# The masked-decay product of a chunked state-space scan: two heads as two 64-column tiles of TensorE's array, in place of zero-padded 128-column weights

## The chip, the cores and the metric

One core of one Trainium2 chip runs the whole program. The metric is the device time of one execution in microseconds (us); the lower, the better. Engines are named as in the profile: PE is TensorE (PEld its weight loads), DVE is VectorE, ACT is ScalarE, POOL is GpSimd, SP is SyncE, which issues nearly all DMAs.

## The reference, cut to what matters

The reference is one layer of a hybrid backbone: a mixer with two branches (a gated linear recurrence, LRU, and a chunked state-space scan, SSD, both in two directions), merged by gates, then a gated MLP with a 3x3 depthwise convolution. The change lies in the SSD branch, in the part of a chunk's outputs that comes from the chunk's own inputs:

```python
# q = 128 tokens a chunk, 8 chunks, 32 heads of 64 channels in 4 groups
decay_in = jnp.exp(segsum(da))
cb = jnp.einsum('bclgn,bcsgn->bgcls', cc, bc)
y_diag = jnp.einsum('bgcls,bgrcls,bcsgrp->bclgrp', cb, decay_in, xdt)
...
y_off = jnp.einsum('bclgn,bcgrpn,bgrcl->bclgrp', cc, prev, jnp.exp(da_cs))
y = (y_diag + y_off).reshape(bsz, seqlen, nh, hp)
```

## The kernel before, in words

Channels lie on partitions, 128 to a tile, and the 1024 tokens along the columns. The large products (`gdense`, L124) split both operands into two parts of type fp32r and take three matmuls of 128x512 for each 128 rows of the contraction. They make nearly all of the program, in all its stages: the LRU stage, then the SSD stage (about 520 to 1230 us of the profile), the merge, and the MLP.

In the SSD stage 16 tiles j of 128 channels, two heads each, go through two generators that are woven together: `ssd_front(j + 1)` makes the next tile's inputs with L124's products, `ssd_back(j)` does the scan of tile j. A scheduler of the framework turns this into one order for each engine; the program text only sets priorities. `ssd_back` consists of:

- `ssd_decay(j, hf)`: for half hf of the tokens (4 chunks c) and each head h, the masked decay matrix `m[:, h, c, :]`, source token on partitions, target token along the columns, both directions in one.
- `ssd_tokens(j)`: the channels xs are transposed on PE (L907, 8 transposes) into PSUM tiles of 4 chunks, and ACT copies them out to `xt`, the tokens on partitions. `xt` has one buffer for all tiles. From it DVE makes `xw`, weighted for the states, which L931 and L932 multiply with `btok`.
- `ssd_y(j, hf)`: the outputs of one half. L982 multiplies `m` with `xt` into `psy`: for each chunk 128 channels by 128 tokens. L990 multiplies the states `S` with `CT`. DVE adds everything into y.

The weights of a PE product are the 128 channels of `xt`; each head has its own `m`, so the two heads can't be one matmul. Before, `xt` has room for two heads of 128 columns, `[NC, 2, P]`; head 0 fills columns 0 to 63 of its room, head 1 columns 64 to 127 of its own, and POOL fills the rest with zeros once (L707). Each head's product then covers all 128 rows of `psy`, and the second adds to the first:

```python
nc.tensor.matmul(psy[:, c, :], self.xt[:, c0 + c, h, :], m[:, h, c, :],
                 start=(h == 0), stop=(h == 1))
```

All of `m`, `xt`, `S` and `CT` are plain fp32, and a plain fp32 product stands in the trace as two pairs of a weight load and a matmul, a product of fp32r as one. Elsewhere in the program, `ada_row` (L314, before 80 us) multiplies with weights of 2 columns, and `token_rs` (L198) sums with a moving operand of one column.

Of the kernel before, what the change touches and what calls it, by code (L numbers as in the profile page):

```python
# [45 lines left out]
class Builder:  # L46
# [28 lines left out]

# [1 line left out]
    def wload(self, src, n=1024, kn=8):  # L77
# [19 lines left out]
    def drain(self):  # L97
        """ahead of the rest: the products wait for this room"""
        return self.tc.high_priority() if self.DRAIN else nullcontext()

    def queue_weights(self, order, ahead):
        """weights in the order of their products; each is loaded `ahead` products early"""
        self.worder, self.wnext, self.wahead, self.wready = order, 0, ahead, {}
# [24 lines left out]
    def halves(self):  # L128
        """room for a product in two halves, from either kind of PSUM tiles in turn"""
        self.turn = not self.turn  # L130
        if self.turn:
            ps = self.t(self.psD, T, "d")
            return [ps[:, :H], ps[:, H:]]
        return [self.t(self.psS, H, "s") for _ in range(2)]

    @staticmethod
    def weave(main, side, ratio):
        """emit `ratio` steps of side for each step of main"""
        acc = 0.0
        nm = ns = 0  # L140
        for _ in main:
            nm += 1
            acc += ratio
            while acc >= 1.0 and side is not None:
                acc -= 1.0
                if next(side, "end") == "end":
                    side = None
                else:
                    ns += 1
        if side is not None:  # L150
            for _ in side:
                ns += 1
        return nm, ns
# [21 lines left out]
    def rsqrt(self, pool, ps, n, inv, tag):  # L175
        """(ps * inv + EPS) ** -0.5 with one Newton step, for few columns"""
        nc = self.nc
        v = self.t(pool, n, tag + "v")
        a = self.t(pool, n, tag + "a")
        r = self.t(pool, n, tag + "r")  # L180
        nc.vector.tensor_scalar(v, ps, inv, EPS, op0=ALU.mult, op1=ALU.add)
        self.act(a, v, AF.Sqrt)
        nc.vector.reciprocal(r, a)
        self.tt(a, r, r)
        self.tt(a, a, v)
        nc.vector.tensor_scalar(a, a, -0.5, 1.5, op0=ALU.mult, op1=ALU.add)
        self.tt(r, r, a)
        return r

    def token_rs(self, pool, parts, n, inv, tag, ps=None):  # L190
        """parts [128, n tokens]: (inv * sum over partitions and parts + EPS) ** -0.5, the tokens on partitions"""
        nc = self.nc
        nch = n // P
        if ps is None:
            ps = self.t(self.psS, nch, "s")
        for c in range(nch):
            for i, q in enumerate(parts):
                nc.tensor.matmul(ps[:, c : c + 1], q[:, c * P : (c + 1) * P], self.ones[:, 0:1],  # L198
                                 start=(i == 0), stop=(i == len(parts) - 1))
        return self.rsqrt(pool, ps[:, :nch], nch, inv, tag)  # L200

    def spread(self, pool, r, out, tag):
        """out[p, c * 128 + t] = r[t, c] for every p"""
        nc = self.nc
        for c in range(r.shape[1]):
            dg = self.t(pool, P, tag + "dg")
            nc.vector.tensor_scalar(dg, self.ident, r[:, c : c + 1], None, op0=ALU.mult)
            nc.tensor.matmul(out[:, c * P : (c + 1) * P], self.ones, dg, start=True, stop=True)

    def log1p01(self, e, d, s, q):  # L210
        """log1p(e) for e in [0, 1], by atanh's series; d, s, q are room for it"""
        nc = self.nc
# [9 lines left out]

# [1 line left out]
    def dt_chain(self, get, x, L, chunk):  # L224
# [32 lines left out]
    def to_tokens(self, src, nch, dst, halves, scale=1.0):  # L257
        """src [128 (d, hf, h), nch * 128] -> dst [128 token, (hf) nch, 16 pair, 4 (d, h2)]"""
        nc = self.nc
# [8 lines left out]

    # ------------------------------------------------------------------ phases
    def setup(self, cpool):  # L270
# [23 lines left out]
    def lam_chain(self, cpool, pool):  # L294
        """-4 * log_sigmoid(lambda) and 8 * log_sigmoid(lambda)"""
        nc = self.nc
# [13 lines left out]
    def ada_row(self, pool, w, scc):  # L310
        """shift and scale of one tile of channels as rows, for x (row 0) and ctx (row 1)"""
        ps = self.t(self.psS, 256, "s")
# [13 lines left out]
    def ada_direct(self, pool, b, w):  # L326
        """the same, the channels on partitions from the start"""
        for s in range(2):
# [10 lines left out]
    def ada_rest(self, p1):  # L339
        """the other shifts, scales and gates, for x alone"""  # L340
        nc, A = self.nc, self.A
# [14 lines left out]
    def modulate(self, t, src, rs, xh, xl, scale, shift):  # L356
        """(src * rs) * scale + shift, split; t is room"""
        self.stt(t, src, scale, rs, op0=ALU.mult, op1=ALU.mult)
        self.act(xh, t, AF.Identity, bias=shift)
        self.stt(xl, t, shift, xh.bitcast(F32), op0=ALU.add, op1=ALU.subtract)  # L360
# [120 lines left out]
    def first(self, cpool):  # L481
        """context, its SSD states, and the LRU branch"""
        nc, tc, A = self.nc, self.tc, self.A
# [121 lines left out]
    def lru_front(self, j):  # L605
        """context in columns 0:256, latents behind"""
        nc, A, p1, p2 = self.nc, self.A, self.q1, self.q2
# [84 lines left out]
    def ssd(self):  # L692
# [6 lines left out]
        with tc.tile_pool(name="sc1", bufs=1) as q1, tc.tile_pool(name="sg1", bufs=1) as g1, \  # L699
# [4 lines left out]
            etb = self.t(q1, [64, NC], "etb")  # L704
            self.xt = self.t(q1, [NC, 2, P], "xt")
            for h in range(2):
                nc.gpsimd.memset(self.xt[:, :, h, 64 - 64 * h : 128 - 64 * h], 0.0)  # L707
            self.tok = (dtt, cst, wtt, cs_d, etb)
# [49 lines left out]
    def load_R(self, j, hf):  # L758
        """the sums of decays for the channels of each head"""
        self.R = self.t(self.p1, [2, H], "R")  # L760
# [7 lines left out]
    def gates_of(self, j):  # L768
        """the gates made with tile j, and after the last tile"""
        mid = 16 - self.EARLY - self.LATE  # L770
# [124 lines left out]
    def ssd_tokens(self, j):  # L895
# [7 lines left out]
        for hf in range(2):  # L903
            ps = self.t(self.psS, [4, P], "s")
            for c in range(4):
                cc = hf * 4 + c
                nc.tensor.transpose(ps[:, c, :], xs[:, cc * P : (cc + 1) * P], self.ident)  # L907
            for h in range(2):
                q = slice(h * 64, h * 64 + 64)
                self.act(xt[:, hf * 4 : hf * 4 + 4, h, q], ps[:, :, q], AF.Copy)  # L910
            yield
        xw = self.t(p1, [2, NC, P], "xw")
        for d in range(2):
            for h in range(2):
                q = slice(h * 64, h * 64 + 64)
                self.tt(xw[:, d, :, q], xt[:, :, h, q],
                        wtt[:, :, j, 2 * d + h : 2 * d + h + 1].to_broadcast([P, NC, 64]))
            yield
        st.update(S=S, xw=xw)

    def ssd_states(self, j):
        """states entering the chunks: direction 0 by rising chunk, direction 1 by falling chunk"""
        nc = self.nc
# [17 lines left out]
    def ssd_decay(self, j, hf):  # L941
        """m: what the inputs of a chunk add to its outputs, both directions in one"""
        dtt, cst = self.tok[:2]
# [25 lines left out]
    def ssd_y(self, j, hf):  # L969
        """outputs of one half of the tokens, the channels on partitions"""  # L970
        nc, p1, p2 = self.nc, self.p1, self.p2
# [8 lines left out]
        for c in range(4):  # L980
            for h in range(2):
                nc.tensor.matmul(psy[:, c, :], self.xt[:, c0 + c, h, :], m[:, h, c, :], start=(h == 0), stop=(h == 1))  # L982
            if c % 2:
# [36 lines left out]
    def merge(self, pA, pM):  # L1020
        """m[k] = ga * (A @ lru_proj) + gb * (B @ ssd_proj), then @ w_out and the first residual."""
        nc, tc, A = self.nc, self.tc, self.A
# [60 lines left out]
    def sumsq(self, pool, ssq, x, m):  # L1083
        """adds to ssq; the last square stays apart"""
        n = x.shape[-1]
# [11 lines left out]
    def norm(self, parts, n, apply, wait):  # L1097
        """1 / rms of n tokens on all partitions, then apply(k, rs) for each tile of channels"""
        p1, p2 = self.p1, self.p2
# [119 lines left out]
    def tail(self, mh, ml, pA, pM, out):  # L1219
        """w_out, first residual and second norm; the channel sub-layer; final norm"""  # L1220
        nc, tc = self.nc, self.tc
# [63 lines left out]
def host_layout(i):  # L1285
    """Host side: slices, transposes and zero padding only."""
    f = lambda a: np.ascontiguousarray(a)
# [69 lines left out]
```

## Time and profile before

| | |
|---|---|
| median of 3 runs | 2357.77 us (2351.71 to 2358.16) |
| profiled execution, span from the first to the last instruction | 2358.4 us |
| PE busy | 2301.8 us, 98% |
| DVE busy | 1617.5 us, 69% |
| ACT busy | 1067.5 us, 45% |
| POOL busy | 3.4 us |
| queue of nearly all DMAs | 249.90 MB, 32.5% of 16 engines |
| chain that ended last | PE 78%, DVE 11%, DMA 5%, ACT 4% |

The profile is one execution, and gives its span alone; its own time is that span, and what lies around it is not listed. Busy time is the union of an engine's instructions. Matmuls are pipelined: their recorded lengths overlap, and their ends are modelled, so a pace is read from starts. "Idle before" is the time for which the engine stood still ahead of a group, with what ended it.

### The profile page before, as it was taken

The page shows a single profiled execution, that of the slowest core. Times are in us where ns is not written, and L with a number is a line of the kernel's source. Part 1 is how long each engine was busy: PE and PEld are TensorE (multiplying, and loading weights), DVE is VectorE, ACT ScalarE, POOL GpSimd, SP SyncE. Part 2 cuts the span into 40 slices and gives each one's busy share as a digit, 9 for nine tenths or more (in the row PEclk, how much of TensorE's full clock was granted, in tenths as well). Part 3 has the DMA queues.
Part 4 walks back from the last instruction along what each step waited for, and adds up shares of the span by engine and source line. Part 5 has one row for each costly group of instructions (what it writes and reads, how often), then busy time and mean ns, then how long its engine had stood idle before and what let it go on. Part 6 is the DMA issues. An engine that isn't in the chain of part 4 may idle for free.

```text
span 2358.4 us, 29544 instructions
## 1 busy us (share of the span) xinstructions
PE 2301.8 (98%) x11530; PEld 1926.7 (82%) x11530; DVE 1617.5 (69%) x2618; ACT 1067.5 (45%) x1633; POOL 3.4 (0%) x16
## 2 busy tenths in 40 slices
PE   7999999999999999999999999999999999999998
PEld 3778878778888888888888878888888888888888
DVE  4877877889978858668876675557765267436655
ACT  4477667677766546646635232333221122112221
POOL 0000000000000000000000000000000000000000
PEclk8999999999999999999999999999999999999999
DMA  6212222144435333423428675532111111111112
GB/s 249 98 60 81 86 83 70 59 128 148 131 100 160 114 119 110 150 83 133 148 92 272 224 240 186 165 100 72 45 53 42 54 49 44 47 53 54 45 54 72
DMA packets 81455, 251.79 MB, mean 107 GB/s; under 512 B 9730, under 2 KB 15906, under 8 KB 76068
## 3 DMA queue, kind: packets, MB, share of 16 engines
q1 hardware_dynamic: 81312, 249.90, 32.5%
q8 instruction: 91, 1.49, 0.3%
q14 instruction: 48, 0.39, 0.1%
q10 hardware_dynamic: 4, 0.01, 0.0%
HBM read 222.33 MB, written 27.54 MB: 106 GB/s over the span
## 4 chain that ended last, share of the span: by engine, by line
PE 78%; DVE 11%; DMA 5%; ACT 4%; issue 2%; DVEq 0%; SPq 0%; ACTq 0%
PE d L124 37%; PE s L124 28%; PE s L982 2%; PE s L990 2%; DMA adar<-in_ada 2%; ACT L L162 2%; PE s L656 2%; DVE wlo L159 1%; DMA gk<-gd 1%; DVE L L159 1%; PE s L931 1%; PE s L932 1%; PE s L314 1%; DVE L L156 1%; DMA raw<-in_w 1%
## 5 line engine op out<-in xcount | busy, mean ns | idle before, releaser
L124 PE MATMUL d<-H,whi 128*128 128x512 f32 x2464 | 690.4, 398 | 1.2 <-ACT whi L162 1.0
L124 PEld LDWEIGHTS d<-H,whi 128*128 128x128 f32 x2464 | 450.6, 188 | 88.7 <-ACT whi L162 1.9
L162 ACT ACTIVATE whi<-raw 128x1024 fp32r<-128x1024 f32 (+1 forms) x194 | 203.2, 1049 | 581.5 <-PE s L124 347.5
L124 PE MATMUL d<-H,wlo 128*128 128x512 f32 x1232 | 385.9, 392 | 0.4 <-DVE wlo L159 0.3
L159 DVE TENSOR_TENSOR wlo<-raw,whi 128x1024 fp32r<-128x1024 f32 (+1 forms) x194 | 234.2, 1209 | 204.3 <-ACT whi L162 201.4
L124 PEld LDWEIGHTS d<-H,wlo 128*128 128x128 f32 x1232 | 230.2, 188 | 49.2 <-DVE wlo L159 1.7
L124 PE MATMUL s<-A,whi 128*128 128x512 f32 x960 | 258.4, 389 | 0.0
L124 PE MATMUL d<-A,whi 128*128 128x512 f32 x960 | 258.3, 389 | 0.0
L124 PE MATMUL s<-H,whi 128*128 128x512 f32 x832 | 251.3, 390 | 0.2 <-ACT whi L162 0.2
L156 DVE SCALAR_TENSOR_TENSOR facc<-d,vec,facc 128x945 f32<-128x945 f32 (+5 forms) x184 | 216.7, 1178 | 11.2 <-ACT facc L162 5.9
L124 PEld LDWEIGHTS d<-A,whi 128*128 128x128 f32 x960 | 180.1, 188 | 37.6
L124 PEld LDWEIGHTS s<-A,whi 128*128 128x128 f32 x960 | 180.2, 188 | 37.3
L124 PEld LDWEIGHTS s<-H,whi 128*128 128x128 f32 x832 | 155.9, 188 | 33.2 <-ACT whi L162 0.7
L162 ACT ACT_TABLE_LOAD x107 | 137.3, 1283 | 76.3 <-DVE cacc L156 28.7
L124 PE MATMUL s<-H,wlo 128*128 128x512 f32 x416 | 157.1, 390 | 2.8 <-DVE wlo L159 2.8
L156 DVE SCALAR_TENSOR_TENSOR M<-s,mods,M 128x512 f32<-128x512 f32 (+1 forms) x72 | 49.6, 690 | 160.7 <-PE s L124 160.5
L124 PE MATMUL d<-A,wlo 128*128 128x512 f32 x480 | 149.2, 389 | 0.2 <-DVE wlo L159 0.2
L124 PE MATMUL s<-A,wlo 128*128 128x512 f32 x480 | 149.1, 389 | 0.0
L124 PEld LDWEIGHTS d<-A,wlo 128*128 128x128 f32 x480 | 90.0, 188 | 19.2 <-DVE wlo L159 0.6
L124 PEld LDWEIGHTS s<-A,wlo 128*128 128x128 f32 x480 | 90.1, 188 | 18.7
L162 ACT ACTIVATE m<-GU,dtt 128x128 f32<-128x128 f32 x256 | 78.9, 389 | 48.5 <-PE s L982 43.5
L156 DVE SCALAR_TENSOR_TENSOR m<-GL,dtt,m 128x128 f32<-128x128 f32 x256 | 77.0, 345 | 29.5 <-ACT m L162 29.0
(274 smaller groups left out, 3191.4 us busy)
## 6 DMA issues: line engine op xcount, KB each, us to landing
raw<-in_w SPq DMA_DIRECT2D x92, 512.0 KB, 3.6
E<-csd SPq DMA_DIRECT2D x32, 1024.0 KB, 4.9
raw<-in_wup SPq DMA_DIRECT2D x44, 512.0 KB, 3.4
R<-csd SPq DMA_DIRECT2D x64, 256.0 KB, 3.9
adar<-in_ada SPq DMA_DIRECT2D x32, 512.0 KB, 4.3
gated<-sg SPq DMA_DIRECT2D x32, 256.0 KB, 2.5
gd<-y SPq DMA_DIRECT2D x32, 256.0 KB, 4.4
gk<-gd SPq DMA_DIRECT2D x32, 256.0 KB, 3.7
```

The lines of the kernel that those rows point to most:

```text
L124: nc.tensor.matmul(o, a[:, k, :], b[k][:, xo + s : xo + e], start=(k == 0 and i == 0), stop=(k == kn - 1 and i == 2))
L156: self.nc.vector.scalar_tensor_tensor(out, in0, s, in1, op0=op0, op1=op1)
L159: self.nc.vector.tensor_tensor(out, a, b, op=op)
L162: self.nc.scalar.activation(out, in_, f, **kw)
L314: self.nc.tensor.matmul(ps[:2, :], scc[:, k, :], w[:, k, :], start=(k == 0), stop=(k == 7))
L656: nc.tensor.matmul(pg, a[:, q, :], b[:, s:e], start=(i == 0), stop=(i == 2))
L931: nc.tensor.matmul(ps[:, s - s2, 0, :], btok[:, s, :], xw[:, 0, s, :], start=True, stop=True)
L932: nc.tensor.matmul(ps[:, s - s2, 1, :], btok[:, 7 - s, :], xw[:, 1, 7 - s, :], start=True, stop=True)
L982: nc.tensor.matmul(psy[:, c, :], self.xt[:, c0 + c, h, :], m[:, h, c, :], start=(h == 0), stop=(h == 1))
L990: nc.tensor.matmul(pso[:, c, :], S[:, cc if d == 0 else 7 - cc, d, :], CT[:, cc * P : (cc + 1) * P], start=True, stop=True)
```

## The change

It puts each head's product on its own half of the array's columns. `xt` shrinks to `[NC, P]`, the two heads side by side, without zeros. Head 0's product has the 64 columns 0 to 63 as weights and writes partitions 0 to 63 of `psy`, head 1's has columns 64 to 127 and writes partitions 64 to 127; neither adds to the other (both start and stop). The framework derives the tile of the array from the operands: 128 rows by 64 columns, at column 0 and at column 64. The copies of `xt` out of PSUM and the products for `xw` no longer go head by head. The changed file also has no comments and docstrings, and from `ssd_y` on its line numbers are 5 lower (L982 becomes L977, L990 becomes L985).

```diff
@@ def ssd
-            self.xt = self.t(q1, [NC, 2, P], "xt")
-            for h in range(2):
-                nc.gpsimd.memset(self.xt[:, :, h, 64 - 64 * h : 128 - 64 * h], 0.0)
+            self.xt = self.t(q1, [NC, P], "xt")
@@ def ssd_tokens
-            for h in range(2):
-                q = slice(h * 64, h * 64 + 64)
-                self.act(xt[:, hf * 4 : hf * 4 + 4, h, q], ps[:, :, q], AF.Copy)
+            self.act(xt[:, hf * 4 : hf * 4 + 4, :], ps, AF.Copy)
             yield
         xw = self.t(p1, [2, NC, P], "xw")
         for d in range(2):
-            for h in range(2):
-                q = slice(h * 64, h * 64 + 64)
-                self.tt(xw[:, d, :, q], xt[:, :, h, q],
-                        wtt[:, :, j, 2 * d + h : 2 * d + h + 1].to_broadcast([P, NC, 64]))
+            self.tt(xw[:, d].rearrange("p c (h q) -> p c h q", h=2), xt.rearrange("p c (h q) -> p c h q", h=2),
+                    wtt[:, :, j, 2 * d : 2 * d + 2].unsqueeze(3).to_broadcast([P, NC, 2, 64]))
             yield
@@ def ssd_y
         for c in range(4):
             for h in range(2):
-                nc.tensor.matmul(psy[:, c, :], self.xt[:, c0 + c, h, :], m[:, h, c, :], start=(h == 0), stop=(h == 1))
+                q = slice(h * 64, h * 64 + 64)
+                nc.tensor.matmul(psy[q, c, :], self.xt[:, c0 + c, q], m[:, h, c, :], start=True, stop=True)
             if c % 2:
                 yield
```

The scheduler makes a new order from this. The number of PE instructions stays the same, 10,568 in the program; ACT has 37 fewer (32 copies, 5 table loads), DVE 32 fewer, POOL 2 fewer, and SP the same 604 DMAs. On PE, the 256 products stand in 36 uninterrupted groups before and after: 28 groups of 8 products, and 4 pairs of groups of 4.

PE, a group of 8 in the middle of the SSD stage (`d` is the PSUM tile of a large product, `s` one of a small product, the shape is that of the output). Before:

```order
2481 L932 MATMUL s_7392<-xw_7274,btok_7091 128x128
2482 L124 MATMUL d_7457<-H_128_481,whi_1037_7296 128x512
2483 L982 MATMUL s_7399<-m_1016_7127,xt_3595 128x128 x8
2484 L124 MATMUL d_7457<-H_129_482,whi_1037_7296 128x512
2485 L990 MATMUL s_7415<-bc_987_6893,S_7258 128x128 x4
```

The same group after the change:

```order
2476 L926 MATMUL s_7354<-xw_7238,btok_7057 128x128
2477 L124 MATMUL d_7419<-H_122_441,whi_1037_7258 128x512 x2
2478 L124 MATMUL d_7419<-H_123_442,whi_1037_7258 128x512
2479 L977 MATMUL s_7361<-m_1016_7093,xt_3595 64x128 x8
2480 L124 MATMUL d_7419<-H_123_442,whi_1037_7258 128x512
2481 L124 MATMUL d_7419<-H_122_441,wlo_1038_7259 128x512 x2
2482 L124 MATMUL d_7419<-H_128_481,whi_1037_7258 128x512
```

The group still stands between two matmuls of L124, that is between products on the whole array; the states' product behind it (L990, now L985) comes three matmuls later.

PE, one of the four places where the group is in two parts. Before:

```order
2408 L124 MATMUL d_7084<-H_122_441,wlo_1000_7020 128x512 x2
2409 L982 MATMUL s_7177<-m_970_6716,xt_3595 128x128 x4
2410 L124 MATMUL d_7084<-H_128_481,whi_999_7019 128x512 x2
2411 L124 MATMUL d_7084<-H_129_482,whi_999_7019 128x512 x2
2412 L124 MATMUL d_7084<-H_128_481,wlo_1000_7020 128x512 x2
2413 L982 MATMUL s_7177<-m_970_6716,xt_3595 128x128 x4
2414 L990 MATMUL s_7193<-bc_809_5256,S_6683 128x128 x4
```

After:

```order
2406 L124 MATMUL d_7050<-H_122_441,wlo_1000_6986 128x512 x2
2407 L977 MATMUL s_7143<-m_970_6682,xt_3595 64x128 x4
2408 L124 MATMUL d_7050<-H_128_481,whi_999_6985 128x512 x2
2409 L124 MATMUL d_7050<-H_129_482,whi_999_6985 128x512 x2
2410 L124 MATMUL d_7050<-H_128_481,wlo_1000_6986 128x512 x2
2411 L977 MATMUL s_7143<-m_970_6682,xt_3595 64x128 x4
2412 L985 MATMUL s_7159<-bc_809_5238,S_6653 128x128 x4
```

Here nothing moved: the two parts stay apart, with the same six matmuls of L124 between them.

## Rows read from the trace of the kernel before

**Rows 1.** The page: span, busy time by engine, PE and its clock by slices.
```profile
span 2358.4 us, 29544 instructions
...
PE 2301.8 (98%) x11530; PEld 1926.7 (82%) x11530; DVE 1617.5 (69%) x2618; ACT 1067.5 (45%) x1633; POOL 3.4 (0%) x16
...
PEclk8999999999999999999999999999999999999999
```
**Rows 2.** Busy time by stretch: PE, PEld, DVE, ACT, POOL, then granted clock, DMA, GB/s.
```profile
520.00:1230.00 710.00, 707.14 (x3952) 609.06 (x3951) 559.22 (x1250) 434.49 (x819) 0.00 (x0) 1.00 0.39 125
...
43.50:58.50 15.00, 15.00 (x74) 7.87 (x73) 10.61 (x18) 5.36 (x9) 0.00 (x0) 1.00 0.72 255
```
**Rows 3.** Waits of PE and PEld, 520 to 1230 us: total us, times, longest.
```profile
PE s L931 <- DVE xw L159: 2.8, 2, 2.2
...
PEld s L931 <- PE d L124: 3.0, 10, 0.9
PEld s L931 <- issue: 2.6, 1, 2.6
```
**Rows 4.** Groups, 520 to 1230 us: count, busy us, mean ns, idle before and releaser.
```profile
L982 PE MATMUL s<-m,xt 128*128 128x128 f32 x512 | 63.0, 275 | 0.0
...
L159 DVE TENSOR_TENSOR xw<-xt,wtt 128x512 f32<-128x512 f32 x60 | 39.0, 681 | 0.0
...
L159 DVE TENSOR_TENSOR m<-m,E 128x1024 f32<-128x1024 f32 x31 | 37.7, 1217 | 0.2
...
L162 ACT ACTIVATE xt<-s 128x256 f32<-128x256 f32 x60 | 19.6, 375 | 23.9 <-PE s L907 23.9
...
L162 ACT ACTIVATE btok<-s 128x512 f32<-128x512 f32 x6 | 3.3, 595 | 1.7 <-PE s L845 1.7
```
**Rows 5.** Timeline of weight loads around one group: start us, length us, engine, line.
```profile
898.52 1.86 PEld L982 LDWEIGHTS s<-m,xt 128*128 128x128 f32 x16
900.30 0.19 PEld L124 LDWEIGHTS d<-H,whi 128*128 128x128 f32 x1
```
**Rows 6.** Timeline around L198: loads, then one of the matmuls.
```profile
884.21 0.41 PEld L124 LDWEIGHTS d<-H,wlo 128*128 128x128 f32 x2
884.75 1.00 PEld L198 LDWEIGHTS s<-ones,ssq 128*128 128x128 f32 x8
885.67 0.77 PEld L124 LDWEIGHTS d<-H,whi 128*128 128x128 f32 x4
...
884.43 0.62 PE L124 MATMUL d<-H,wlo 128*128 128x512 f32 x2
```
**Rows 7.** Timeline of PE where L314 and L124 alternate.
```profile
44.47 3.62 PE L314 MATMUL s<-adaw,scc 128*2 128x256 f32 x16
48.02 0.60 PE L323 MATMUL s<-ident,row 2*128 2x2 f32 x4
...
50.40 0.73 PE L124 MATMUL d<-H,whi 128*128 128x512 f32 x2
51.06 0.59 PE L314 MATMUL s<-adaw,scc 128*2 128x256 f32 x2
51.59 0.73 PE L124 MATMUL d<-H,whi 128*128 128x512 f32 x2
52.25 1.02 PE L314 MATMUL s<-adaw,scc 128*2 128x256 f32 x4
53.21 0.73 PE L124 MATMUL d<-H,whi 128*128 128x512 f32 x2
```
**Rows 8.** L864 and L982, each line's loads: length ns min/median/max, first and last start.
```profile
L864 PEld LDWEIGHTS s<-ident,grsr x4: 84/84/84, 686.1 to 1242.6; 128*8 128x8 f32 x4
...
L982 PEld LDWEIGHTS s<-m,xt x512: 186/192/192, 522.1 to 1226.3; 128*128 128x128 f32 x171
```
**Rows 9.** The chain in order of time: start, us, line and count.
```profile
1441.14 10.88 PE d L124 x48
```
**Rows 10.** Timeline of weight loads at one switch, idle time before in brackets.
```profile
51.06 0.09 PEld L314 LDWEIGHTS s<-adaw,scc 128*2 128x2 f32 x2 [0.37 <-issue]
```

## The prediction

> **What bounds the kernel now.** I read the page first: TensorE (PE) is busy for 2301.8 of 2358.4 us, and its clock digits stand at 9 nearly throughout [rows 1]. A busy PE is not proof that PE is the bound, so the next view is the stretch in which the changed lines run. All of L982, L907's copies and the xw products lie between 520 and 1230 us. There PE is busy for 707.14 of 710 us at a granted clock of 1.00, which is the 2.4 GHz level, VectorE (DVE) for 559 and ScalarE (ACT) for 434 [rows 2]. The third view is the waits of PE in that stretch: the reader is to see that the matmuls waited twice on DVE's xw, 2.8 us in all, and the loads of L931 for 5.6 us more, in pieces [rows 3]. So in this stage a microsecond of PE work taken away or added is a microsecond of the end, until DVE (79% busy) becomes the bound. Behind the stage lie about 1130 us of other products, which the change does not touch.
>
> **What one group costs before.** The groups of instructions give L982 512 matmuls of 128x128 [rows 4], and its line 512 weight loads [rows 8]. The program has 256 such products (16 tiles, 2 halves, 4 chunks, 2 heads), so each fp32 product is recorded as two pairs of a load and a matmul. The recorded lengths (275 and 192 ns) overlap, so I take the pace from starts: 16 loads from 898.52 to 900.30 us, 0.111 us per pair [rows 5]. The whole product costs 512 x 0.111 = 56.8 us of PE.
>
> What sets 0.111? Two things at once. L198 has the same 128-column load and a matmul of a single column, and still goes 8 pairs from 884.75 to 885.67, 0.115 each [rows 6]: the load alone sets the pace. L314 is the reverse, 2 columns of weights and 256 columns streamed: groups of 2, 4 and 16 take 0.53 (51.06 to 51.59), 0.96 (52.25 to 53.21) and 3.55 us (44.47 to 48.02) [rows 7]; the slope, (3.55 - 0.53) / 14, is 0.216 us for 256 columns, so 0.108 for 128. Load and stream both take what is seen, and halving the load alone gains next to nothing. The clock was 1.00 there too [rows 2].
>
> **The change, part by part.**
> (a) The product. After the change each load has 64 columns. Of the load I take half of 0.111, 0.056 us; the lengths of an 8-column and a 128-column load, 84 and 192 ns [rows 8], are 0.9 ns a column apart, which says 0.053. The stream still has 128 columns, 0.108 us. So everything hangs on whether the two heads, now on two halves of the columns, stream side by side. The trace has no two matmuls on different column tiles; the bounds are full overlap and none. In the order of the program each chunk is head 0 twice, then head 1 twice. If a matmul waits only for its own half, the second of head 0 runs beside the first of head 1, and the second of head 1 beside the first of the next chunk: two streams' time a chunk, 0.216 us, against four loads, 0.224. Paced by the loads, 512 x 0.056 = 28.7 us, and at the end of each of 36 groups the last stream sticks out by 0.05, 1.9 us: 30.6, a gain of 26.2. Without overlap it is 512 x 0.108 = 55.3, a gain of 1.5. I take full overlap, because nothing in the rows makes the second half wait and the loads ran under the streams in L314's small tile, 16 in the 3.55 us that the streams alone explain [rows 7].
>
> The Trainium skill has a measurement for this in TensorE: Matmul & The Clock Gate, Part 3, "Measured speedup vs the span model": three column tiles at 2.38 times the pace of one. No run here shows it; for two tiles it would give nearly the sum above.
>
> (b) The switches. L982's groups now use half the array's columns at a time, the products around them all of it. The trace has such switches where L314 (2 columns of weights) alternates with L124. From the first L124 matmul at 50.40 to the first at 51.59 us are 1.19 us [rows 7]; a 512-column matmul takes 10.88 / 48 = 0.227 us [rows 9], so two of these and two of L314 are 0.886, and 0.304 is left. The next round, 51.59 to 53.21 with four of L314, leaves 1.62 - 0.454 - 0.864 = 0.302. The row of loads shows why: L314's load begins at 51.06 together with its matmul, and the loader sat idle before it [rows 10]; between products of one kind the load is ahead, L124's at 884.21 for a matmul at 884.43 [rows 6]. L864 looks like a counter-example (8 columns, no gap), but it is a transpose and its compiled load still names the whole array, so it prices nothing. To 0.304 I add the 64-column load that is now exposed on entering, 0.056: 0.36 us for in and out. The order lists 36 groups, before and after, each with full-array products on both sides: 36 x 0.36 = 13.0 us lost. The bounds are nothing (a switch that falls where the loader waits anyway) and these 13.0.
>
> (c) xt is copied out of PSUM by one ACT instruction of 512 columns for each half, not two of 256. Before, 4 x 0.375 us for each tile; a 512-column copy takes 0.595 (btok) [rows 4], so 1.50 becomes 1.19, 5.0 us of ACT over 16 tiles. The order has 5 table loads fewer as well. xw is two DVE instructions of 1024 instead of four of 512: 4 x 0.681 = 2.72 becomes 2 x 1.217 = 2.43 [rows 4], 4.6 us. PE hides both: ACT and DVE are at 61% and 79% of the stage [rows 2], and the one wait of PE that this can shorten is the 2.8 us on xw [rows 3]. I count nothing. If the cover goes (PE gains 26 us) DVE's share is still 555 of 684 us, 81%. POOL's two fills of xt lie before the stage and nobody waits for them. The DMAs are the same 604; on SP the scheduler moves R and E loads by a few places, and E's lateness costs ACT time that PE does not see.
>
> **Sum.** -26.2 + 13.0 = -13.2 us against the profiled execution's span of 2358.4, so 2345. The median of the runs, 2357.77, stands 0.03% under that span; I make no correction.
>
> **The rivals.**
> *No overlap.* The heads stream one after the other: -1.5 + 13.0 = +11.5 us, 2370. This is slower, by one mechanism, the switches around 36 groups; it decides as soon as the overlap saves under 13.0 us, 0.36 us for each of the 36 groups. It is also the case in which the change doesn't do what it says. For it: no row shows two tiles at once. Against it: nothing in the rows ties the halves together.
> *Half overlap.* If a load only begins when the matmul before it has started (in [rows 5] loads and matmuls keep one pace), head 1's first matmul starts 0.056 after head 0's second, and its own second a stream later: 2 x (0.108 + 0.056) = 0.328 a chunk, 42.0 us for 128 chunks, a gain of 14.8 and a net -1.8: 2357, no change. For it: loads and matmuls pair off one to one in the rows. Against it: a half that is free could be loaded earlier.
> *Free switches.* Full overlap, and the gap hidden by waits that the loader has anyway: -26, 2332. Against it: both rounds of [rows 7] give the gap, 0.304 and 0.302.
> *Exposed loads.* In the tile mode the load no longer runs under the stream: 512 x (0.108 + 0.056) = 84.0, +27.2, and with the switches +40, 2398. Against it: L314's 16 in 3.55 us. The Trainium skill, in the same page's Part 3, "The mechanism", says loads overlap running matmuls only where the row groups differ; both heads use all rows, so by that rule this rival would come true. L314's row group is also all rows and its loads are hidden, so the trace disagrees, though its loads are of 2 columns.
>
> **How the numbers follow.** Full overlap 0.42, half overlap 0.24, no overlap 0.20, free switches 0.09, exposed loads 0.05. The likeliest gives 2345; its own range, with switches between a third and all of their price and the loads at 0.053 to 0.06, is 2335 to 2348. For 8 in 10 the range runs from 2333 (nearly free switches) to 2372 (no overlap, with 2 us for the moved order). A measurement of this kernel can tell about 0.3%, 7 us, from no change. Faster by more: most of full overlap and free switches, 0.46. Within: half overlap mostly, with edges of its neighbours, 0.28. Slower: no overlap and exposed loads, 0.26.
>
> **What would show each step.** In the changed profile L982's line has become L977, with 512 matmuls of 64 columns of weights. The starts of a group of 16 decide: 0.9 us and what the switch adds for full overlap, 1.3 for half, 1.73 for none, 2.6 for exposed loads. A load after a group (L124's) that begins some 0.2 us after the last L977 matmul started, not with it, shows the switch; the pair costs 0.36 us if I am right. PE must still be busy throughout 520 to 1230, and the stage shorter by 13 us; a new wait of PE on xw, S or m there, or a stage that ends earlier with the end unmoved, would make the forecast wrong in another way.

## The result and the profile after

The changed kernel takes 2339.78 us in the median of 4 runs (2339.40 to 2342.84), the kernel before 2357.40 in 4 runs beside them: a ratio of 0.9936 (95% interval 0.9922 to 0.9950), 17.6 us in the medians. Two later sets of runs gave 2340.69 (0.9926, 0.9915 to 0.9938) and 2339.57 (0.9929, 0.9913 to 0.9945). The forecast was 2345, its range 2333 to 2372. The profiled execution has a span of 2341.1 us against 2358.4, 17.3 us less.

The page of the changed kernel: span, busy time by engine, the granted clock in 40 slices, and the engines' shares of the chain that ended last.

```profile
span 2341.1 us, 29454 instructions
...
PE 2285.2 (98%) x11530; PEld 1896.3 (81%) x11530; DVE 1613.5 (69%) x2586; ACT 1061.3 (45%) x1596; POOL 2.4 (0%) x14
...
PEclk8999999999999999999999999999999999999999
...
PE 84%; DVE 10%; DMA 3%; ACT 2%; issue 1%; DVEq 0%; ACTq 0%
```

PE has 16.6 us less to do (2301.8 in [rows 1]) and the span is shorter by about as much. So the time was taken from PE's work, and PE still leads the chain (84% of it).

Busy time in the SSD stage, the columns as in [rows 2], and what PE and its loads still waited for there.

```profile
520.00:1230.00 710.00, 707.99 (x4039) 592.68 (x4038) 561.38 (x1231) 434.81 (x794) 0.00 (x0) 1.00 0.41 129
```
```profile
PE s L198 <- DVE ssq L159: 1.0, 1, 1.0
PE s L925 <- DVE xw L159: 0.6, 1, 0.6
...
PEld s L977 <- issue: 11.2, 32, 0.4
PEld d L124 <- issue: 5.3, 31, 0.2
```

PE is as full as before, at a clock of 1.00. No wait of PE on another engine is over 1.0 us. New are the last two rows: the loader stands idle ahead of nearly every group of L977 (11.2 us, 32 times) and ahead of the product behind it (5.3 us, 31 times). These are the switches.

The loads of L977 (length in ns: least, median, most; then first and last start), and the groups of the stage.

```profile
L977 PEld LDWEIGHTS s<-m,xt x512: 132/137/137, 520.2 to 1206.3; 128*64 128x64 f32 x171
```
```profile
L977 PE MATMUL s<-m,xt 128*64 128x128 f32 x512 | 35.9, 280 | 0.0
...
L159 DVE TENSOR_TENSOR xw<-xt,wtt 128x1024 f32<-128x1024 f32 x30 | 36.4, 1222 | 0.6 <-ACT xt L162 0.6
...
L162 ACT ACTIVATE xt<-s 128x512 f32<-128x512 f32 x30 | 17.5, 593 | 29.8 <-PE s L905 29.8
```

From the first load of the product to the last are now 686.1 us, against 704.2 (522.1 to 1226.3) in [rows 8]: 18.1 us, all of the gain, lie in the stage. L977's 512 matmuls cover 35.9 us, L982's covered 63.0 [rows 4]. The copies and xw came out as costed: 593 ns a copy where 595 was taken, 1222 ns an xw product where 1217 was.

What one group costs can be read where it stands in the same company in both kernels, between two and four matmuls of L124. PE's timeline (start us, length us, engine, line, count), before:

```profile
910.94 0.62 PE L124 MATMUL d<-H,wlo 128*128 128x512 f32 x2
911.40 1.95 PE L982 MATMUL s<-m,xt 128*128 128x128 f32 x16
913.10 1.17 PE L124 MATMUL d<-H,whi 128*128 128x512 f32 x4
914.10 0.62 PE L124 MATMUL d<-H,wlo 128*128 128x512 f32 x2
```

After, matmuls and then loads (in brackets the loader's idle time before):

```profile
896.80 0.61 PE L124 MATMUL d<-H,wlo 128*128 128x512 f32 x2
897.34 1.09 PE L977 MATMUL s<-m,xt 128*64 128x128 f32 x16
898.37 1.20 PE L124 MATMUL d<-H,whi 128*128 128x512 f32 x4
899.40 0.62 PE L124 MATMUL d<-H,wlo 128*128 128x512 f32 x2
...
897.34 0.85 PEld L977 LDWEIGHTS s<-m,xt 128*64 128x64 f32 x16 [0.35 <-issue]
898.37 0.76 PEld L124 LDWEIGHTS d<-H,whi 128*128 128x128 f32 x4 [0.17 <-issue]
```

From the first start to the last are 3.16 us before (910.94 to 914.10) and 2.60 after (896.80 to 899.40). Six matmuls of L124, 6 x 0.227 [rows 9], are 1.36 of both, so the group costs 1.80 before and 1.24 after: 0.56 us saved. Within the group the recorded starts after the change come in pairs, 7 ns between the two of a pair; from the first pair to the second are 0.16 us, from there on 0.109 to 0.110 from pair to pair. At 0.110 the 8 pairs are 0.88 us. What is left, 0.36 by these rounded starts and 0.355 as the median over the groups of 16 that have four matmuls of L124 behind them, is the switch: 0.09 us more than usual between L124's last start and L977's first, 0.05 in the longer first step inside the group, and some 0.2 on the way out, where the load of L124 only begins with its own matmul (898.37 both). The experiments below were planned with 0.345.

Over the stage: 28 groups of 16 at a median of 0.564 us make 15.8, 8 groups of 8 at 0.091 make 0.7. That is 16.5 of the 17.3 us.

### The profile page after: what moved, and what is told of

It is laid out like the page before. It is cut to its first block, busy times and chain, and to the rows that moved or that the text cites. A ratio compares the mean times of both kernels' runs of the same rounds, so it can differ in the third digit from the quotient of the medians.

```text
span 2341.1 us, 29454 instructions
## 1 busy us (share of the span) xinstructions
PE 2285.2 (98%) x11530; PEld 1896.3 (81%) x11530; DVE 1613.5 (69%) x2586; ACT 1061.3 (45%) x1596; POOL 2.4 (0%) x14
## 4 chain that ended last, share of the span: by engine, by line
PE 84%; DVE 10%; DMA 3%; ACT 2%; issue 1%; DVEq 0%; ACTq 0%
PE d L124 42%; PE s L124 30%; PE s L985 2%; PE s L656 2%; PE s L977 1%; DVE wlo L159 1%; DVE L L159 1%; PE s L926 1%; DMA adar<-in_ada 1%; PE s L925 1%; ACT L L162 1%; PE s L314 1%; DVE L L681 1%; DMA raw<-in_w 1%; PE s L598 1%
## 5 line engine op out<-in xcount | busy, mean ns | idle before, releaser
L124 PE MATMUL d<-H,whi 128*128 128x512 f32 x2464 | 690.4, 398 | 0.4 <-ACT whi L162 0.2
L124 PEld LDWEIGHTS d<-H,whi 128*128 128x128 f32 x2464 | 451.0, 189 | 93.5 <-issue 6.0
L124 PE MATMUL d<-H,wlo 128*128 128x512 f32 x1232 | 386.5, 393 | 2.0 <-DVE wlo L159 2.0
L124 PEld LDWEIGHTS d<-H,wlo 128*128 128x128 f32 x1232 | 229.9, 188 | 51.5 <-DVE wlo L159 3.7
L124 PE MATMUL s<-A,whi 128*128 128x512 f32 x960 | 258.4, 389 | 0.0
L124 PE MATMUL d<-A,whi 128*128 128x512 f32 x960 | 258.3, 389 | 0.0
L124 PE MATMUL s<-H,whi 128*128 128x512 f32 x832 | 252.5, 391 | 2.7 <-ACT whi L162 2.7
L156 DVE SCALAR_TENSOR_TENSOR facc<-d,vec,facc 128x945 f32<-128x945 f32 (+5 forms) x184 | 216.8, 1178 | 11.2 <-ACT facc L162 5.9
L124 PEld LDWEIGHTS d<-A,whi 128*128 128x128 f32 x960 | 180.2, 188 | 37.6
L124 PEld LDWEIGHTS s<-A,whi 128*128 128x128 f32 x960 | 180.2, 188 | 37.3
L124 PEld LDWEIGHTS s<-H,whi 128*128 128x128 f32 x832 | 156.6, 189 | 36.0 <-ACT whi L162 3.1
L124 PE MATMUL s<-H,wlo 128*128 128x512 f32 x416 | 157.4, 391 | 1.4 <-DVE wlo L159 1.3
L124 PE MATMUL s<-A,wlo 128*128 128x512 f32 x480 | 149.2, 389 | 0.5 <-DVE wlo L159 0.5
L124 PE MATMUL d<-A,wlo 128*128 128x512 f32 x480 | 149.1, 389 | 0.0
L124 PEld LDWEIGHTS s<-A,wlo 128*128 128x128 f32 x480 | 90.0, 188 | 19.5 <-DVE wlo L159 1.0
L124 PEld LDWEIGHTS d<-A,wlo 128*128 128x128 f32 x480 | 90.1, 188 | 18.7
L156 DVE SCALAR_TENSOR_TENSOR E<-E,cst 128x128 f32<-128x128 f32 x256 | 82.3, 349 | 19.5 <-ACT E L162 19.5
```

What stands on the lines that cost most here:

```text
L124: nc.tensor.matmul(o, a[:, k, :], b[k][:, xo + s : xo + e], start=(k == 0 and i == 0), stop=(k == kn - 1 and i == 2))
L156: self.nc.vector.scalar_tensor_tensor(out, in0, s, in1, op0=op0, op1=op1)
```

## The experiments

The theory: the two tiles' streams run side by side (8 stream times for a group of 16 matmuls), each of the 36 groups pays one switch of some 0.35 us, and nothing else counts. Its rivals give the gain to the shorter chains on ACT and DVE, let the two fp32 passes of one product overlap instead of the two heads, or hold that the switches cost nothing. The first four kernels that follow shared one chip and 29 runs of the kernel before (median 2356.41).

### e1: the product alone

The kernel before, with its padded xt, its copies and its xw, and only the product on the tiles:

```diff
-                nc.tensor.matmul(psy[:, c, :], self.xt[:, c0 + c, h, :], m[:, h, c, :], start=(h == 0), stop=(h == 1))
+                q = slice(h * 64, h * 64 + 64)
+                nc.tensor.matmul(psy[q, c, :], self.xt[:, c0 + c, h, q], m[:, h, c, :], start=True, stop=True)
```

> The kernel before with the product alone changed: xt keeps its zero-padded room, its copies and xw go head by head, and only the two matmuls of a chunk take 64 columns each and write 64 partitions. Theory (the two heads' streams run side by side, each group of 16 matmuls in about 0.88 us, less about 0.35 us of switch for each of 36 groups): all of the gain is here, 2340 us give or take 3. Rival (the gain is in the copies, in xw or in the scheduler's new order): 2352 to 2358, as before.

Measured: 2338.05 us (2336.19 to 2344.46), ratio 0.9926 (0.9912 to 0.9939). The groups of this kernel's stage:

```profile
L159 DVE TENSOR_TENSOR xw<-xt,wtt 128x512 f32<-128x512 f32 x60 | 39.3, 684 | 0.0
...
L983 PE MATMUL s<-m,xt 128*64 128x128 f32 x496 | 34.8, 280 | 0.0
L983 PEld LDWEIGHTS s<-m,xt 128*64 128x64 f32 x496 | 26.4, 136 | 12.0 <-issue 10.7 <-ACT m L162 1.1
```

The xw products are the old ones of 512 columns, the matmuls the new ones, and the loader has the same idle time ahead of them. The whole gain is there without the shorter chains on ACT and DVE.

### e2: the copies and xw alone

The changed kernel with the product on the whole array:

```diff
-                nc.tensor.matmul(psy[q, c, :], self.xt[:, c0 + c, q], m[:, h, c, :], start=True, stop=True)
+                nc.tensor.matmul(psy[:, c, :], self.xt[:, c0 + c, :], m[:, h, c, :], start=True, stop=True)
```

> The changed kernel with the product back on the whole array: each head multiplies with all 128 columns of xt, and head 1 overwrites head 0 (so head 0's decay is left out of the result); the compact xt, its single copies and the two xw instructions stay. Theory: no gain without the tiles, 2357 give or take 3, matmuls 0.112 us apart, a load beginning with the last matmul of a group. Rival (copies, xw or order carry the gain): 2340.

Measured: 2354.55 us (2350.37 to 2358.59), ratio 0.9988 (0.9979 to 0.9996), 1.9 us less in the medians. PE's timeline at a group:

```profile
904.08 1.95 PE L976 MATMUL s<-m,xt 128*128 128x128 f32 x16
905.78 1.17 PE L124 MATMUL d<-H,whi 128*128 128x512 f32 x4
```

From 904.08 to 905.78 are 1.70 us, as before the change (911.40 to 913.10). On whole-array products the shorter chains are worth at most a few us: the waits of PE on xw, 2.8 us in [rows 3], were gone in this kernel's stage. But e1 had no such wait either, with the old chains, so the part does not add to the product's.

### e3: all of head 0, then all of head 1

The changed kernel with its two loops exchanged:

```diff
-        for c in range(4):
-            for h in range(2):
-                q = slice(h * 64, h * 64 + 64)
+        for h in range(2):
+            q = slice(h * 64, h * 64 + 64)
+            for c in range(4):
                 nc.tensor.matmul(psy[q, c, :], self.xt[:, c0 + c, q], m[:, h, c, :], start=True, stop=True)
-            if c % 2:
-                yield
+            yield
```

> The changed kernel with the loops of the product exchanged: first head 0 for four chunks, then head 1 for four, the same 64-column tiles and the same number of groups and switches. Theory (overlap needs a matmul of the other tile near in the order): the 16 matmuls go one after the other at 0.109, 1.7 us a group, 2340 + 32 x 0.8 = 2366, slower than before. Rival (two recorded matmuls of one product, not two tiles, run side by side, or the engine fetches the other head's matmuls out of order): 2340, the pairs unchanged.

Measured: 2357.00 us (2353.46 to 2360.95), ratio 1.000 (0.9989 to 1.001): between the two expectations. PE's timeline:

```profile
889.70 1.58 PE L977 MATMUL s<-m,xt 128*64 128x128 f32 x16
891.21 0.50 PE L124 MATMUL d<-H,whi 128*128 128x512 f32 x1
```

From 889.70 to 891.21 are 1.51 us; after the change it was 1.03 (897.34 to 898.37). The order within the group alone takes back the gain: 0.48 us for a group of 16. The starts within this group, in ns from one to the next, are

```
160 109 109 110 5 104 56 53 57 52 57 109 109 109 109
```

Matmuls of one head follow one another a full stream apart (109), so the rival that the two passes of one product overlap is out: the overlap is between the tiles. Eight groups of this kernel hold one head alone; there the starts are 109 or 110 apart throughout, behind a first step of 160, and nothing overlaps: 8 matmuls take the 1.09 us in which the changed kernel has 16.

```profile
655.44 1.09 PE L977 MATMUL s<-m,xt 128*64 128x128 f32 x8
```

But my theory in its strict form is out as well. In the order of the program head 1's first matmul is the ninth; had every matmul waited for the one ahead of it to start, the group's last would start 1.64 us after its first (15 x 0.109), and it starts after 1.31. With eight 109-ns streams on each tile, a body this short needs head 1 to begin beside head 0's fifth, ahead of three that still wait. That is read from the times, since the records do not name the tile. In the middle both run (starts 52 to 57 ns apart), then head 0 runs out, and head 1 finishes alone. So the other half of the rival, that the other head's matmuls are started out of order, holds in part.

### e4: more switches

The states' matmul of one direction is put behind each chunk's two products, so the groups on the tiles become 80 short ones instead of 36, with the same matmuls. Against the changed kernel:

```diff
+        pso = self.t(self.psS, [4, P], "s")
         for c in range(4):
             for h in range(2):
...
+            cc = c0 + c
+            nc.tensor.matmul(pso[:, c, :], S[:, cc, 0, :], CT[:, cc * P : (cc + 1) * P], start=True, stop=True)
```

> The changed kernel with the first states' product of each half (L985, direction 0) put between the chunks of the masked product: in 16 of the 32 halves the order now has four tile groups with a whole-array product between them, 80 groups instead of 36, and no other work. Theory (a switch in and out costs about 0.345 us whatever stands around it): 44 x 0.345 = 15 us more, and 1 to 2 us for streams that lose their partner at a group's end, 2340 + 16 = 2356. Rival (the gaps of rows 7 belong to the early stage, a switch is nearly free here): 2340 to 2343.

Measured: 2355.10 us (2352.03 to 2356.86), ratio 0.9991 (0.9983 to 1.000). PE's timeline (L978 is the product on the tiles, L980 the states' product):

```profile
901.65 0.44 PE L978 MATMUL s<-m,xt 128*64 128x128 f32 x4
902.01 0.49 PE L980 MATMUL s<-bc,S 128*128 128x128 f32 x2
902.43 0.44 PE L978 MATMUL s<-m,xt 128*64 128x128 f32 x4
902.80 0.49 PE L980 MATMUL s<-bc,S 128*128 128x128 f32 x2
903.22 0.44 PE L978 MATMUL s<-m,xt 128*64 128x128 f32 x4
```

A round takes 0.785 us (901.65 to 903.22 is two). Two pairs on the tiles are 0.22, two matmuls of L980 another 0.22, so 0.345 us is the switch in and out. By the times, the kernel is 15.3 us above the changed kernel's 2339.78; over 44 added groups that is 0.35 us each. The two ran on different chips; by the two ratios (0.0055 of 2356.4) it is 0.29, and against e1 on the same chip (2338.05) 0.39. The rival of free switches would have left the time where it was. With 80 groups nearly all of the gain is gone.

### e6 and e7: both halves of a tile in one group

If each switch costs 0.35 us, fewer and longer groups should gain. e6 puts the products of both halves of the tokens together, behind the next tile's first decay, so that 36 groups become 17. m gets a third buffer for that, and y takes psy in before the second direction's states, to save room in PSUM. The diff against the changed kernel, in ssd_back and ssd_y, cut to its core:

```diff
-    BUFS = {"L": 10, "adaw": 3, "raw": 2, "cacc": 4, "csg": 2, "row": 3, "xdg": 4}
+    BUFS = {"L": 10, "adaw": 3, "raw": 2, "cacc": 4, "csg": 2, "row": 3, "xdg": 4, "m0": 3}
...
+            yield from self.ssd_y(j - 1, 0)
             yield from self.ssd_y(j - 1, 1)
...
-        yield from self.ssd_y(j, 0)
...
+        if hf == 0:
+            st["psy"] = {}
+            for g in (0, 1):
+                st["psy"][g] = self.t(self.psS, [4, P], "s")
...
+            self.tt(y, t[:, 1] if d else psy.rearrange("p c q -> p (c q)"), y if d else t[:, 0], op=ALU.add)
```

> The changed kernel with the outputs of both halves of a tile made together, after the next tile's first decay matrix (a third buffer for m; the masked product of 8 chunks stands in one piece; y takes the product's part before the second states' product): 17 groups in the order where there were 36, the same work. Theory (each group pays about 0.345 us for its switches): 19 x 0.345 = 6.6 us less, 2333. Rival (what a group pays is given back elsewhere, or the moved outputs make PE wait): 2339 to 2345.

Measured: 2341.53 us (2338.64 to 2343.61), ratio 0.9929 (0.9917 to 0.9941), against 2340.69 for the changed kernel on the same chip: no gain, a miss. The waits in its stage, the timeline of ACT and PE at one of them, and the busy times and clock there (columns as in [rows 2]):

```profile
PE d L124 <- ACT zs L162: 6.4, 3, 2.7
...
PEld s L981 <- issue: 5.0, 14, 0.4
...
ACT xs L162 <- DVE y L156: 17.9, 8, 4.7
```
```profile
869.21 1.21 ACT L162 ACTIVATE xs<-d,vec 128x1024 f32<-128x1024 f32 x1 [3.58 <-DVE y L156]
...
871.72 1.02 ACT L162 ACTIVATE zs<-d 128x1024 f32<-128x1024 f32 x1
...
872.80 1.24 PE L124 MATMUL d<-H,whi 128*128 128x512 f32 x4 [2.73 <-ACT zs L162]
...
874.70 1.91 PE L124 MATMUL d<-H,whi 128*128 128x512 f32 x4
876.40 1.01 PE L124 MATMUL d<-H,wlo 128*128 128x512 f32 x2
```
```profile
873.00:877.00 4.00, 4.00 (x12) 3.15 (x12) 3.06 (x4) 3.95 (x5) 0.00 (x0) 0.60 0.16 18
```

The switches went as meant: the loader's idle time ahead of the product fell from 11.2 to 5.0 us. But three times PE now waits for ACT, which has to empty a large product's PSUM tile into zs, 6.4 us in all. ACT comes late because ahead of zs, in its own order, it stands idle until DVE has made y (3.58 us here, 17.9 in the stage where the changed kernel has 1.0). That y reads the tile of xs made before, and ACT is about to write the next xs: the later outputs hold xs longer. After the longest of PE's waits the granted clock stands at 0.60 in the mean of the next 4 us: the four matmuls from 874.70 take until 876.40, 0.425 each instead of 0.227. What the fewer switches should have saved, 6.6 us, is about what these waits and the slow matmuls behind one of them took.

e7 has e6's move, with the product on the whole array as in e2, so that there are no switches to save; against e6:

```diff
-                        q = slice(h * 64, h * 64 + 64)
-                        nc.tensor.matmul(st["psy"][g][q, c, :], self.xt[:, g * 4 + c, q], st["m"][g][:, h, c, :],
+                        nc.tensor.matmul(st["psy"][g][:, c, :], self.xt[:, g * 4 + c, :], st["m"][g][:, h, c, :],
                                          start=True, stop=True)
```

> The same move of the outputs with the product on the whole array, as in the run that kept the copies only (head 0's decay is left out of the result). Theory: without tiles there is no switch to save, so the move alone gives nothing, 2353 to 2357. Rival (the move itself helps or hurts): 2347 or less, or 2362 or more.

Measured: 2370.17 us (2366.22 to 2378.27), ratio 1.0053 (1.0039 to 1.0067). Busy times in its stage, and its waits:

```profile
520.00:1230.00 710.00, 699.27 (x3837) 602.55 (x3836) 543.56 (x1183) 409.74 (x763) 0.00 (x0) 0.99 0.38 121
```
```profile
PE d L124 <- ACT zs L162: 6.7, 3, 2.2
PE s L906 <- ACT xt L162: 2.7, 3, 2.2
```

PE stands still for 10.7 of the 710 us, 2.9 before the change [rows 2]; the profile is of the slowest of the six runs (2378.27 us). The theory that the move alone gives nothing failed, and the rival that it hurts holds: 12 us in the medians. The price is not one constant, though: with these 12 us and 6.6 saved e6 would stand 5.8 us above the changed kernel, and it stands 0.8 above. So e6's miss is accounted for by the waits in its own trace; e7 shows that the move can hurt, and neither confirms nor refutes the price of a switch.

### e8: heads in turn, two chunks at a time

e3 suggests that the other tile's matmul must stand near in the order. Here, in the changed kernel, two chunks of head 0 are followed by two of head 1:

```diff
-        for c in range(4):
+        for b in range(0, 4, 2):
             for h in range(2):
                 q = slice(h * 64, h * 64 + 64)
-                nc.tensor.matmul(psy[q, c, :], self.xt[:, c0 + c, q], m[:, h, c, :], start=True, stop=True)
-            if c % 2:
-                yield
+                for c in range(b, b + 2):
+                    nc.tensor.matmul(psy[q, c, :], self.xt[:, c0 + c, q], m[:, h, c, :], start=True, stop=True)
+            yield
```

> The changed kernel with two chunks of head 0, then two of head 1, in turn, so that four recorded matmuls of one tile stand ahead of four of the other. Theory (from the run with four chunks a head, where head 1's first matmul started beside head 0's fifth of eight, past three that still waited): three can be passed, so the tiles still run side by side throughout, 2340 give or take 2. Rival (a matmul of the other tile passes no more than one that waits, and the half overlap of that run has another cause): half of the loss of that run or more, 2348 to 2357.

Measured: 2342.81 us (2340.64 to 2343.83), ratio 0.9933 (0.9920 to 0.9946), on the chip where the changed kernel took 2340.69. PE's timeline:

```profile
896.12 1.15 PE L978 MATMUL s<-m,xt 128*64 128x128 f32 x16
897.20 1.20 PE L124 MATMUL d<-H,whi 128*128 128x512 f32 x4
```

That is 0.8 us above the theory's range and well below the rival's 2348. The group takes 1.08 us to the next start instead of 1.03. Four matmuls of one head in a row, where e3 had eight, are bridged almost wholly. As in e3, waiting matmuls of head 0 are passed by those of head 1.

### e9: both halves together, but not where PSUM ran out

e6's waits fell near 670, 870 and 1070 us, at the tile that begins a new group of heads. e9 leaves tiles 3, 7 and 11 as in the changed kernel: 20 groups. The diff against e6, cut to its core:

```diff
+            if jj:
+                yield from self.ssd_y(j - 1, 0)
...
+        if jj == 3 and j < XS_TILES - 1:
+            yield from self.ssd_y(j, 0)
...
+        apart = j % 4 == 3 and j < XS_TILES - 1
+        if hf == 0 or apart:
+            st["psy"] = {}
+            for g in (hf,) if apart else (0, 1):
```

> The kernel with both halves' outputs together, except for tiles 3, 7 and 11, whose outputs stay where the change has them: the tile after each of them begins a group, and there the earlier version's PE waited for PSUM room (three waits of 2.2 to 3.1 us, and eight or more matmuls at half pace behind one). 20 groups in place of 36. Theory (0.345 us a group, and the loss of the earlier version was those waits): 16 x 0.345 = 5.5 us less than the changed kernel, 2335 give or take 2. Rival (the waits come back at other tiles): 2339 to 2343.

Measured: 2332.56 us (2331.59 to 2342.15), ratio 0.9907 (0.9890 to 0.9925) against 2356.54 before; the changed kernel, on the same chip, 2339.57. The page, the loads' waits in the stage, and PE's timeline at a group:

```profile
span 2329.9 us, 29461 instructions
...
PE 2275.6 (98%) x11530; PEld 1894.9 (81%) x11530; DVE 1610.2 (69%) x2586; ACT 1058.5 (45%) x1596; POOL 2.4 (0%) x14
```
```profile
PEld s L985 <- issue: 5.7, 16, 0.4
PEld d L124 <- issue: 3.4, 20, 0.2
```
```profile
886.17 0.61 PE L124 MATMUL d<-H,wlo 128*128 128x512 f32 x2
886.72 1.97 PE L985 MATMUL s<-m,xt 128*64 128x128 f32 x32
888.61 1.20 PE L124 MATMUL d<-H,whi 128*128 128x512 f32 x4
889.65 0.62 PE L124 MATMUL d<-H,wlo 128*128 128x512 f32 x2
```

The median is 0.4 us under the theory's 2333 to 2337, and PE has no wait on another engine in this stage. From 886.17 to 889.65 are 3.48 us; less six matmuls of L124, a group of 32 costs 2.12 us, where two groups of 16 cost 1.24 each: 0.36 us less, one switch. Sixteen switches fewer at 0.345 are 5.5 us; the medians differ by 7.0, the spans by 7.5 (2337.4 for the changed kernel in that set), so some 2 us come from elsewhere in the moved order, which no run separates. It is the fastest kernel of this study by its median and its span, but the intervals of the two ratios overlap (0.9890 to 0.9925, and 0.9913 to 0.9945) and two of its six runs took 2337.20 and 2342.15: the saving is shown at the group, and in the time it is not clear of the spread.

## Why the prediction was right, and where it was off

**What bounds the kernel.** Right. PE's work fell by 16.6 us and the span by 17.3, with PE at 707.99 of 710 us in the stage. No other engine took over.

**(a) The product, full overlap.** Right in the mechanism, and this is what the forecast rested on. No row of the kernel before showed two tiles at once: full overlap was a choice between two bounds, with a chance of 0.42, and that it came true is in part luck. The 0.9 us that it asked of the starts in a group are 0.82 from first to last. Paced by the loads at 0.056 us, with a last stream that sticks out by 0.05 at 36 groups, it gave 30.6 us; this is the term that was mis-sized. The streams set the pace: 0.110 us for a pair, in which both tiles' loads fit, and the same 0.109 where e3 runs one head alone with half as many loads. So the product is 256 x 0.110 = 28.2 us. I had paired the second matmul of head 0 with the first of head 1, which leaves a lone stream at each end. The recorded starts are pairs from the first to the last, which fits the two heads' first passes starting together. The product before the change was also a little dearer than 0.111 x 512: 1.80 a group where 16 x 0.111 is 1.78.

**(b) The switches.** Right: against 0.36 us once for each group stand 0.355 by the timeline, 0.345 by e4's rounds and 0.29 to 0.39 by e4's time. The sign for which I looked, a load behind the group that begins with its own matmul and not before, is in the row at 898.37.

**(c) Copies and xw counted as nothing.** Right for this change, since e1 without them is as fast. Alone on the old product they gave 1.9 us (0.9 to 4.9 by the interval), about the waits on xw that [rows 3] shows, so "nothing" holds only beside the other part.

**The sum.** Forecast -13.2, found -16.5 by the groups. Of the 3.3 us between, 1.9 are the tail, which was counted on top of the switch, 0.5 the pace of the product, 0.2 the switch, and the rest the dearer product before. What belongs to a tail and what to the switch is bookkeeping: 0.41 us a group were forecast for both together, 0.355 are measured, and no run separates them.

**The rivals.** *No overlap* (2370) and *half overlap* (2357) fall by the pairs of starts. e3 came out at the half-overlap rival's time, 2357, but by another way: full overlap in the middle of the group and none at its ends. The rival's reason, that a load waits for the matmul before it to start, would have held for the change's order too, where it does not show. *Free switches* (2332) falls by e4. *Exposed loads* (2398) falls by the timeline: 16 loads of 64 columns lie within the 0.88 us that eight streams take. By the Trainium skill (TensorE: Matmul & The Clock Gate, Part 3, "The mechanism") a load overlaps running matmuls only if its row group differs, so loads on the same rows would have been exposed. This case's trace disagrees, now for loads of 64 columns as well as for the 2 columns of [rows 7]; the same section also lets a load into the background weight buffer go ahead, which would allow what is seen, though no run here shows that buffer. The Trainium skill's 2.38 times for three column tiles (TensorE: Matmul & The Clock Gate, Part 3, "Measured speedup vs the span model") stands beside 1.80 / 0.88, 2.0 times for two tiles here without the switches, and 1.45 times (1.80 / 1.24) with them. The prediction said that the 2.38 would give nearly its sum for two tiles. That does not follow: two thirds of 2.38 are 1.6 times, an estimate from that figure, and the sum has 56.8 / 30.6, 1.86 times.

## What to carry to other kernels

Two products that each fill half of the array's columns, on the same rows, run side by side at the full two times in plain fp32, loads included, if the order alternates between the two tiles within a few matmuls; all of one and then all of the other lost the whole gain in e3. Each stay on the tiles costs one switch in and out, about 0.35 us here, so a group should be long: eight pairs of streams save 0.9 us and pay 0.35, while the 0.22 us that two pairs save do not pay for it. Before such groups are moved together, see which buffers the move holds longer: in e6 the waits behind a longer held xs took about what the switches saved.

## What was not expected of the hardware

A matmul on one tile starts ahead of waiting ones on the other, though not of any number of them. e3's body of 1.31 us, against 1.64 in strict order, fits a start past three waiting matmuls; the depth is worked out from the starts of this one pattern and from e8's, and no run varied it by itself. And a wait of PE can cost more than its length: behind the 2.73 us on zs in e6, matmuls of L124 took 0.425 us instead of 0.227, in a stretch with a mean granted clock of 0.60.
